# Attention scores of two heads in the two row halves of the TensorE array, with one PSUM bank left for transpositions

## The chip, the cores and the metric

The kernel runs on one core of a Trainium2 chip, as one program with one launch. The metric is the time of an execution on the device in microseconds (us), lower is better. Engines are named as in the profile: PE is TensorE's matmul, PEld its weight load, DVE is VectorE, ACT is ScalarE, POOL is GpSimd and SP is SyncE, which issues the DMAs.

## The reference, cut to what matters

The program is one layer of a diffusion backbone: 1024 latent tokens and 256 context tokens of width 1024 go through an input projection into two token mixers (a bidirectional mLSTM and windowed attention), a gated merge, and a ConvFFN. The change is in the attention:

```python
# 16 query heads, 4 key/value heads, head width 64; blocks of T = 128 queries
s_lat = einsum('btkgd,bskd->bkgts', qblk, kblk) * ATT_SCALE   # 3 blocks of keys around the query block
s_lat = where(valid, s_lat, NEG_INF)                          # |i - j| <= 128
s_ctx = einsum('btkgd,bskd->bkgts', qblk, k_ctx) * ATT_SCALE  # all 256 context keys
p = softmax(concatenate([s_lat, s_ctx, sink_b], axis=-1))[..., :3*T + C]
out = p_lat @ v_lat + p_ctx @ v_ctx
```

## The kernel before

Everything is fp32. A product of two fp32 matrices is made from rounded parts: a value x is split into a high part that the matmul takes exactly (type fp32r) and the remainder, and the products of the parts are added up. In most of the kernel that is three products (high by high, high by low, low by high; `mm3`, L95 to L97 and `filler`, L692).

**The attention's loop.** 32 blocks (4 key/value heads g, 8 query blocks b each) go through a software pipeline, one step n for each. A step issues `proj` of block n (24 products, 384 columns, tile `pq`), `stacks` of block n-1 (transposes q and k, tile `qt`), `scores` of block n-3 (tile `s`), and `pv` of block n-4. `filler` gives each step 24 products of 512 columns of another projection (tile `g`), which need nothing from the attention, and which are put between the steps' other products. The order on each engine is made by a list scheduler when the program is built, not by the order of the source.

**Scores.** The head width is 64, so `stacks` puts the high part of q into one half of the 128 rows and the low part into the other half (`QT`, four heads of 128 columns), while the keys stand twice, once in each half (`KA` the high parts, `KB` the low parts; `KcA` and `KcB` for the context). A matmul over all 128 rows then gives (high q + low q) by one part of the keys, and two of them give all four products. Per head:

```python
595  for h in range(4):
596      ps = s_tile(f"s{n}_{h}")
597      q = QT[:, h * P : (h + 1) * P]
599          nc.tensor.matmul(ps[:, off:512], q, KA[:, b0 * P : b1 * P], start=True, stop=False)
600          nc.tensor.matmul(ps[:, off:512], q, KB[:, b0 * P : b1 * P], start=False, stop=True)
601          nc.tensor.matmul(ps[:, 512 : 512 + NCTX], q, KcA[:, g], start=True, stop=False)
602          last = nc.tensor.matmul(ps[:, 512 : 512 + NCTX], q, KcB[:, g], start=False, stop=True)
```

The latent keys are 384 columns wide (256 in the first and the last block of a head group), the context keys 256. One DVE instruction per head then scales, masks and finds the maximum (L606, reading `s` from PSUM), ACT takes the exponential (L610), and POOL normalises (L619).

**Probabilities by values.** `pv` transposes the probabilities of four heads for one block of 128 keys into one PSUM bank (four matmuls against the identity, L639, tile `pt`); `split_from` copies the bank to `ph` on ACT (L44) and subtracts on DVE to get `pl` (L49); both must have read the bank before it can be written again. Then two products (L633 with `ph`, L634 with `pl`) add to `po`. A block has five such key blocks (four at the ends).

**PSUM.** There are eight banks of 512 columns. Before, `mm_tile` has two, `fl_tile` (the filler) one, `tp_tile` (all transpositions: `qt`, `pt`, and a small one for the modulation, `ms`) three, and `s_tile` two, which hold one head's scores.

Of the kernel before, what the change touches and what calls it, by code (L numbers as in the profile page):

```python
# [8 lines left out]
F32 = mybir.dt.float32  # L9
F32R = mybir.dt.float32r  # L10
AF = mybir.ActivationFunctionType
ALU = mybir.AluOpType
# [87 lines left out]
def sl(a, n):  # L100
    return slice(a, a + n)
# [3 lines left out]
def layer_kernel(ctx: ExitStack, tc: tile.TileContext, A: dict, out: bass.AP, dbg=None):  # L105
# [28 lines left out]
    pss = psx_s.enter_context(tc.tile_pool(name="ps_s", bufs=1, space=PSUM, reuse_waits="tile"))  # L134
    ph1 = ExitStack()
# [12 lines left out]

    def tp_tile(name):
        return pst.tile([P, 512], F32, tag="tp", name=name)  # L150

    def s_tile(name):
        return pss.tile([P, 1024], F32, tag="s", name=name)

# [5 lines left out]
        attT_d=attT_d, mlT_d=mlT_d, sga_d=sga_d, sgm_d=sgm_d, kx_d=kx_d, vx_d=vx_d, sil3=sil, sil=sil[:, :, 0], dbg=dbg,  # L160
        mm_tile=mm_tile, fl_tile=fl_tile, tp_tile=tp_tile, s_tile=s_tile, psx_s=psx_s,
# [82 lines left out]
def attention_setup(E, st):  # L244
    nc, tc, A = E.nc, E.tc, E.A
    ap = st.enter_context(tc.tile_pool(name="at1", bufs=1, reuse_waits="tile"))
    at = Ctx()
    maskA = ap.tile([P, 640], F32, name="maskA")
    mask7 = ap.tile([P, 512], F32, name="mask7")
    nsink = ap.tile([P, 16], F32, name="nsink")  # L250
# [9 lines left out]
    def tables(cs):  # L260
        nc.sync.dma_start(cs, A["rope"].rearrange("(b p) c -> p b c", p=P))
        nc.sync.dma_start(sink, A["sink"].to_broadcast([P, 16]))
        nc.sync.dma_start(E.gb, A["gate_b"].to_broadcast([P, 16]))
        nc.sync.dma_start(maskA, A["maskA"])
        nc.sync.dma_start(mask7, A["mask7"])
# [12 lines left out]
    Vc = ap.tile([P, NCB, NKV, P], F32R, name="Vc")  # L278
    at.__dict__.update(maskA=maskA, mask7=mask7, nsink=nsink, sink=sink, qw=qw, TA=TA, TB=TB, KcA=KcA, KcB=KcB, Vc=Vc, constants=constants, tables=tables)
    return at  # L280
# [221 lines left out]
def stage_attention(E, st, at):  # L502
    nc, tc, A, ident, expo, hT, wts, vecT = E.nc, E.tc, E.A, E.ident, E.expo, E.hT, E.wts, E.vecT
    mm_tile, tp_tile, s_tile, attT_d = E.mm_tile, E.tp_tile, E.s_tile, E.attT_d
    maskA, mask7, nsink, sink, TA, TB = at.maskA, at.mask7, at.nsink, at.sink, at.TA, at.TB
    KcA, KcB, Vc = at.KcA, at.KcB, at.Vc
# [51 lines left out]
    def stacks(g, b):  # L558
        n = f"{g}_{b}"
        qf, ss = S1.pop((g, b))  # L560
        kf = wp.tile([P, 2, HD], F32, tag="kf", name=f"kf{n}", bufs=2)
        nc.vector.tensor_scalar(kf, qf[:, None, 256:320].to_broadcast([P, 2, HD]), ss[:, 4:5], None, op0=ALU.mult)


        pt = tp_tile(f"qt{n}")
        for i in range(2):
            nc.tensor.transpose(pt[:, i * P : (i + 1) * P], qf[:, i * P : (i + 1) * P], ident)
        nc.tensor.transpose(pt[:, 256:384], kf.rearrange("p r d -> p (r d)"), ident)
        QT = wp.tile([P, 512], F32R, tag="QT", name=f"QT{n}", bufs=3)
        Q4 = QT.rearrange("p (i r t) -> p r i t", i=2, r=2)  # L570
        pq = pt[:, 0:256].rearrange("p (i t) -> p i t", i=2)
        halves = slice(0, HD), slice(HD, P)
# [5 lines left out]
        for r in range(2):  # L578
            hi, lo = halves[r], halves[1 - r]
            nc.vector.tensor_tensor(Q4[lo, r], pq[hi], Q4[hi, r].bitcast(F32), op=ALU.subtract)  # L580
        nc.vector.tensor_tensor(G[g]["KB"][:, ts], pt[:, 256:384], G[g]["KA"][:, ts].bitcast(F32), op=ALU.subtract)
        S2[(g, b)] = (QT, ss)

    def scores(g, b):
# [4 lines left out]
        W = nl + NCTX  # L589
        off = 512 - nl  # L590
        mask = maskA[:, 128:640] if b == 0 else (mask7 if b == NB - 1 else maskA)
        KA, KB = G[g]["KA"], G[g]["KB"]
        st4 = wp.tile([P, 16], F32, tag="st", name=f"st{n}", bufs=4)
        Ps, prior = [], None
        for h in range(4):
            ps = s_tile(f"s{n}_{h}")
            q = QT[:, h * P : (h + 1) * P]
            with behind(prior):
                nc.tensor.matmul(ps[:, off:512], q, KA[:, b0 * P : b1 * P], start=True, stop=False)
                nc.tensor.matmul(ps[:, off:512], q, KB[:, b0 * P : b1 * P], start=False, stop=True)  # L600
                nc.tensor.matmul(ps[:, 512 : 512 + NCTX], q, KcA[:, g], start=True, stop=False)
                last = nc.tensor.matmul(ps[:, 512 : 512 + NCTX], q, KcB[:, g], start=False, stop=True)  # L602
            prior = FILL.products(6) if h in (0, 1, 2) else None
            pm = pp.tile([P, 640], F32, tag="P", name=f"P{n}_{h}", bufs=8)
            hh = 4 * g + h
            nc.vector.tensor_tensor_reduce(  # L606
                pm[:, :W], ps[:, off : off + W], mask[:, :W], scale=ss[:, h : h + 1], scalar=nsink[:, hh : hh + 1],
                op0=ALU.add, op1=ALU.min, accum_out=st4[:, h : h + 1],
            )
            nc.scalar.activation(  # L610
                pm[:, :W], pm[:, :W], AF.Exp, bias=st4[:, h : h + 1], scale=-1.0, accum_out=st4[:, 4 + h : 5 + h]
            )
            Ps.append(pm)
        nc.vector.tensor_tensor(st4[:, 8:12], st4[:, 0:4], sink[:, 4 * g : 4 * g + 4], op=ALU.add)
# [3 lines left out]
        for h in range(4):  # L618
            nc.gpsimd.tensor_scalar(Ps[h][:, :W], Ps[h][:, :W], st4[:, 12 + h : 13 + h], 1.0, op0=ALU.mult, op1=ALU.mult)  # L619
        S3[(g, b)] = (Ps, b0, b1)  # L620

    def pv(g, b):
# [13 lines left out]
        for kb in range(nk):  # L636
            pt = tp_tile(f"pt{n}_{kb}")
            for h in range(4):
                turned = nc.tensor.transpose(pt[:, h * P : (h + 1) * P], Ps[h][:, kb * P : (kb + 1) * P], ident)  # L639
            ph = pp.tile([P, 512], F32R, tag="ph", name=f"ph{n}_{kb}", bufs=3)  # L640
# [93 lines left out]
def stage_mlstm(E, st):  # L734
    nc, tc, A, ident, expo, hT, wts, dr = E.nc, E.tc, E.A, E.ident, E.expo, E.hT, E.wts, E.dr
    mm_tile, tp_tile, s_tile, mlT_d, gtile = E.mm_tile, E.tp_tile, E.s_tile, E.mlT_d, E.gtile

    E.psx_s.close()
    psd = E.psx_s.enter_context(tc.tile_pool(name="ps_d", bufs=2, space=PSUM, reuse_waits="tile"))
    E.d_tile = lambda name: psd.tile([P, 512], F32, tag="d", name=name)  # L740
    mp = st.enter_context(tc.tile_pool(name="ml1", bufs=1, reuse_waits="tile"))
# [248 lines left out]
    def states(h):  # L990
# [5 lines left out]
        def update(d, i, c):  # L996
# [7 lines left out]
            nc.vector.scalar_tensor_tensor(kl, ks[c], wk, kh.bitcast(F32), op0=ALU.mult, op1=ALU.subtract)  # L1004
            pd = psd.tile([P, 512], F32, tag="d", name=f"dC{nm}")
            mm3(nc, pd[:, :DVA], [(kh, kl)], [VA[c]], sl(0, P), sl(0, DVA))
# [160 lines left out]
def stage_tail(E, st):  # L1167
# [342 lines left out]

    psc = E.psx_s
    U = Units(
# [16 lines left out]
    with tc.issue_after(held.ins):  # L1529
        w = load_w(A["w_o"][1], "wo1", g1b[:, 512:1024], raws=raw)  # L1530
    E.psx_s.close()
    psc = st.enter_context(tc.tile_pool(name="ps_c", bufs=2, space=PSUM, reuse_waits="tile"))
    E.c_tile = lambda n: psc.tile([P, 512], F32, tag="C", name=n)
    for b in range(4):
# [397 lines left out]
def host_arrays(inp):  # L1932
# [56 lines left out]
    z = np.zeros((P, P))  # L1989
    a["maskA"] = np.concatenate([prev, z, nxt, z, z], axis=1).astype(np.float32)  # L1990
    a["mask7"] = np.concatenate([prev, z, z, z], axis=1).astype(np.float32)
    fw = np.where(i[:, None] <= i[None, :], 0.0, NEG)
# [21 lines left out]
```

## Time and profile before

| | us |
|---|---|
| median of 3 runs | 1909.65 (1908.51 to 1911.2) |
| the profiled execution, its own time | 1909.96 |
| its span in the trace | 1908.2 |
| attention's stretch of the span (all 32 blocks) | about 130 to 640 |

The span is what the trace shows between the first and the last instruction; the execution's own time is 1.76 us longer. A timeline row has its start (us from the span's start), its length, engine, line, operation, the tile written and those read, and a count where rows were merged (then the length is that of all of them). Matmuls overlap: the distance between two starts is what one costs, and the length of one is longer.

### The profile page before, as it was taken

To read this page: it belongs to the slowest core of one execution; us is meant where nothing else is said; L and a number is where in the kernel's file an instruction comes from. 1 tells how busy PE (TensorE), PEld (TensorE's weight loads), DVE (VectorE), ACT (ScalarE), POOL (GpSimd) and SP (SyncE) were. 2 spreads that over 40 slices of the span, in tenths; PEclk is the share of its full clock that TensorE was granted. 3 is DMA by queue.
4 is the path that set the end of the run, shared out by engine and by line. 5 is a ranking of instruction groups with operands and counts; after the bars stand their busy time and mean duration, and the time that the engine had idled before them with its cause. 6 is when DMAs were issued, how large, how long until landed. Compare 5 with 4: busy or idle time off the path is not lost.

```text
span 1908.2 us, 28768 instructions
## 1 busy us (share of the span) xinstructions
PE 1880.6 (99%) x10021; PEld 1631.5 (86%) x10021; DVE 1434.3 (75%) x2892; ACT 998.1 (52%) x1984; POOL 306.5 (16%) x524
## 2 busy tenths in 40 slices
PE   7999999999999999999999999999999999999999
PEld 3898888989888899999988887888888888888887
DVE  3767878877677766667577878679888889897565
ACT  4845656555556445454546665276544444455441
POOL 1223333333333231212020012000000000000000
PEclk9999999999999999999999999999999999999999
DMA  9632222322122433435318973613355444499851
GB/s 355 197 121 75 67 72 67 103 61 84 59 64 83 129 92 119 133 125 166 133 56 291 383 263 127 237 67 110 135 201 188 185 165 174 164 320 347 305 165 67
DMA packets 139570, 298.54 MB, mean 156 GB/s; under 512 B 15504, under 2 KB 39968, under 8 KB 136608
## 3 DMA queue, kind: packets, MB, share of 16 engines
q1 hardware_dynamic: 125024, 270.48, 40.9%
q10 hardware_dynamic: 14400, 26.22, 4.0%
q8 instruction: 79, 1.29, 0.3%
q14 instruction: 67, 0.55, 0.1%
HBM read 220.55 MB, written 76.10 MB: 155 GB/s over the span
## 4 chain that ended last, share of the span: by engine, by line
PE 89%; DVE 4%; ACT 2%; DMA 2%; POOL 2%; issue 1%; POOLq 0%; SPq 0%; ACTq 0%; DVEq 0%
PE g L692 9%; PE pa L1591 4%; PE pa L1593 4%; PE pa L1592 4%; PE pt L639 3%; PE pq L95 2%; PE pq L96 2%; PE yb L1593 2%; PE yb L1592 2%; PE pq L97 2%; PE yb L1591 2%; PE kv L96 2%; PE kv L95 2%; PE kv L97 2%; PE dx L1593 2%; PE po L633 2%
## 5 line engine op out<-in xcount | busy, mean ns | idle before, releaser
L619 POOL TENSOR_SCALAR P<-P,st 128x640 f32<-128x640 f32 (+1 forms) x128 | 106.7, 852 | 222.6 <-DVE st L617 80.3
L610 ACT ACTIVATE P<-P,st 128x640 f32<-128x640 f32 (+1 forms) x128 | 102.8, 803 | 58.6 <-DVE st L606 58.6
L606 DVE CUSTOM_DVE_ANT_0 P<-s,maskA,nsink 128x640 f32<-128x640 f32 (+1 forms) x112 | 103.0, 920 | 22.2 <-PE s L602 20.6
L49 DVE TENSOR_TENSOR pl<-pt,ph 128x512 fp32r<-128x512 f32 x152 | 100.6, 684 | 4.5 <-ACT ph L44 3.3
L44 ACT ACTIVATE ph<-pt 128x512 fp32r<-128x512 f32 x152 | 86.2, 595 | 30.9 <-PE pt L639 29.5
L692 PE MATMUL g<-hH,fh 128*128 128x512 f32 x256 | 101.2, 395 | 0.0
L692 PE MATMUL g<-hH,fl 128*128 128x512 f32 x256 | 100.6, 393 | 0.0
L692 PE MATMUL g<-hL,fh 128*128 128x512 f32 x256 | 100.2, 391 | 0.0
L95 PE MATMUL pq<-w1h,hH 128*128 128x384 f32 (+1 forms) x256 | 87.0, 340 | 0.1
L97 PE MATMUL pq<-w1h,hL 128*128 128x384 f32 (+1 forms) x256 | 86.9, 339 | 0.0
L639 PE MATMUL pt<-ident,P 128*128 128x128 f32 x608 | 86.4, 272 | 0.3 <-POOL P L619 0.3
L96 PE MATMUL pq<-w1l,hH 128*128 128x384 f32 (+1 forms) x256 | 86.4, 338 | 0.0
L639 PEld LDWEIGHTS pt<-ident,P 128*128 128x128 f32 x608 | 72.3, 140 | 10.0 <-POOL P L619 0.5
L95 PE MATMUL mo<-w1h,hH 128*128 128x256 f32 x256 | 72.0, 281 | 0.0
L1729 ACT ACTIVATE cv<-ua,vecT 128x1024 f32<-128x1024 f32 x22 | 27.4, 1244 | 85.0 <-DVE ua L1702 85.0
L97 PE MATMUL mo<-w1h,hL 128*128 128x256 f32 x256 | 71.8, 280 | 0.0
L96 PE MATMUL mo<-w1l,hH 128*128 128x256 f32 x256 | 71.8, 280 | 0.0
L1003 POOL TENSOR_SCALAR kwh<-k,gcall 128x128 fp32r<-128x128 f32 x72 | 32.4, 454 | 237.6 <-PE dC L96 189.0
L96 PE MATMUL kv<-w1l,hH 128*128 128x384 f32 x208 | 70.2, 338 | 0.0
L97 PE MATMUL kv<-w1h,hL 128*128 128x384 f32 x208 | 70.0, 337 | 0.0
L95 PE MATMUL kv<-w1h,hH 128*128 128x384 f32 x208 | 70.0, 337 | 0.0
L1591 PE MATMUL dx<-dwh,dfh 128*128 128x512 f32 (+1 forms) x176 | 68.3, 388 | 0.0
(600 smaller groups left out, 6405.1 us busy)
## 6 DMA issues: line engine op xcount, KB each, us to landing
ur<-in_w_up SPq DMA_DIRECT2D x22, 1024.0 KB, 4.9
wmb<-in_w_modB SPq DMA_DIRECT2D x48, 256.0 KB, 2.8
f_d<-cv SPq DMA_DIRECT2D x22, 512.0 KB, 2.6
wm<-in_w_modA SPq DMA_DIRECT2D x16, 512.0 KB, 10.2
fr<-in_w_g SPq DMA_DIRECT2D x32, 256.0 KB, 3.1
drf<-fs_d SPq DMA_DIRECT2D x15, 512.0 KB, 7.1
drw<-wt_d SPq DMA_DIRECT2D x14, 512.0 KB, 6.4
w1b<-in_w_cx SPq DMA_DIRECT2D x16, 388.0 KB, 5.1
```

What stands on the lines that cost most here:

```text
L49: rest = nc.vector.tensor_tensor(lo, src, hi.bitcast(F32), op=ALU.subtract)
L95: nc.tensor.matmul(ps, lh[:, ls], rh[:, rs], start=start and i == 0, stop=False)
L96: nc.tensor.matmul(ps, lh[:, ls], rl[:, rs], start=False, stop=False)
L97: nc.tensor.matmul(ps, ll[:, ls], rh[:, rs], start=False, stop=stop and i == n - 1)
L606: nc.vector.tensor_tensor_reduce(pm[:, :W], ps[:, off : off + W], mask[:, :W], scale=ss[:, h : h + 1], scalar=nsink[:, hh : hh + 1], op0=A ...
L610: nc.scalar.activation(pm[:, :W], pm[:, :W], AF.Exp, bias=st4[:, h : h + 1], scale=-1.0, accum_out=st4[:, 4 + h : 5 + h])
L619: nc.gpsimd.tensor_scalar(Ps[h][:, :W], Ps[h][:, :W], st4[:, 12 + h : 13 + h], 1.0, op0=ALU.mult, op1=ALU.mult)
L639: turned = nc.tensor.transpose(pt[:, h * P : (h + 1) * P], Ps[h][:, kb * P : (kb + 1) * P], ident)
L692: return lambda: nc.tensor.matmul(ps, w, x, start=i == 0, stop=i == len(todo) - 1)
L1591: nc.tensor.matmul(ps, lh, rh, start=start and i == 0, stop=False, skip_group_check=True)
L1592: nc.tensor.matmul(ps, lh, rl, start=False, stop=False, skip_group_check=True)
L1593: nc.tensor.matmul(ps, ll, rh, start=False, stop=stop and i == n - 1, skip_group_check=True)
```

## The change

`QT` now holds the high parts of all four heads (columns 0 to 255) and their low parts (256 to 511), with head 2i in rows 0 to 63 and head 2i+1 in rows 64 to 127. One ACT copy and one DVE subtraction over 128 rows make it, where there were two of each over 64 rows. A score matmul is over 64 rows: head 2i uses rows 0 to 63 of the array, head 2i+1 rows 64 to 127. Each head has three products per key part (low by low is left out), so a pair of heads has 12 matmuls, which alternate between the two halves, where two heads had 8 over 128 rows. The two heads write to different banks: `s_tile` is now four banks, for a pair. `tp_tile` is left with one bank in the attention; outside of it the two banks that this frees are a second pool (`third`), and `tp_tile` turns through three banks as before. The order of the key parts in the first and the last block, and the masks (one table for two), are changed to suit. The filler is given out 12 products after the first pair, where it was six after each of three heads.

```diff
-    pst = psx.enter_context(tc.tile_pool(name="ps_tp", bufs=3, space=PSUM, reuse_waits="tile"))
+    pst = psx.enter_context(tc.tile_pool(name="ps_tp", bufs=1, space=PSUM, reuse_waits="tile"))
...
+    def banks(tag, n, bufs, third):
+        psx_s.close()
+        pool = psx_s.enter_context(tc.tile_pool(name=f"ps_{tag}", bufs=bufs, space=PSUM, reuse_waits="tile"))
+        setattr(PS, tag, lambda name: pool.tile([P, n], F32, tag=tag, name=name))
+        PS.third, PS.turn = None, 0
+        if third:
+            PS.third = psx_s.enter_context(tc.tile_pool(name=f"ps_{tag}t", bufs=2, space=PSUM, reuse_waits="tile"))
...
+            banks("s", 2048, 1, False)
             stage_attention(E, st, at)
...
-        for r in range(2):
-            hi, lo = halves[r], halves[1 - r]
-            copy_act(nc, Q4[hi, r], pq[hi])
+        copy_act(nc, QT[:, 0:256], pt[:, 0:256])
...
-        for h in range(4):
-            ps = s_tile(f"s{n}_{h}")
-            q = QT[:, h * P : (h + 1) * P]
+        for i in range(2):
+            ps = s_tile(f"s{n}_{i}")
+            work = []
+            for r, (al, ac, _) in enumerate(places):
+                rows = sl(r * HD, HD)
+                qh, ql = QT[rows, sl(i * P, P)], QT[rows, sl(256 + i * P, P)]
+                both = []
+                for at_, w, (ka, kb) in (
+                    (al, nl, (KA[rows, lat], KB[rows, lat])),
+                    (ac, NCTX, (KcA[rows, g], KcB[rows, g])),
+                ):
+                    both.append([(ps[:, at_ : at_ + w], q, k) for q, k in ((qh, ka), (ql, ka), (qh, kb))])
+                work.append(both[0] + both[1])
             with behind(prior):
-                nc.tensor.matmul(ps[:, off:512], q, KA[:, b0 * P : b1 * P], start=True, stop=False)
...
+                for j in range(6):
+                    for r in range(2):
+                        o, q, k = work[r][j]
+                        nc.tensor.matmul(o, q, k, start=j % 3 == 0, stop=j % 3 == 2)
-            prior = FILL.products(6) if h in (0, 1, 2) else None
+            prior = FILL.products(12) if i == 0 else None
```

The scheduler makes a new order from this. In the rows below `s_3_0` is the first tile of scores of query block 3 of the third head group (before: its first head; now: its first pair), `pt_2_1` the transposed probabilities of query block 2 for its second block of keys, `ph` and `pl` their two parts, `g` the filler and `pq` the next projection.

On PE, before, from the last transposition of the first key block on: with three banks the sets of transpositions stand side by side.

```order
L639 MATMUL pt_2_0_5093<-ident,P_2_3_4892 128x128
L639 MATMUL pt_2_1_5102<-ident,P_2_0_4856 128x128
L639 MATMUL pt_2_1_5102<-ident,P_2_1_4870 128x128
L639 MATMUL pt_2_1_5102<-ident,P_2_2_4884 128x128
L639 MATMUL pt_2_1_5102<-ident,P_2_3_4892 128x128
L639 MATMUL pt_2_2_5111<-ident,P_2_0_4856 128x128
L639 MATMUL pt_2_2_5111<-ident,P_2_1_4870 128x128
L639 MATMUL pt_2_2_5111<-ident,P_2_2_4884 128x128
L639 MATMUL pt_2_2_5111<-ident,P_2_3_4892 128x128
L633 MATMUL po_2_5092<-ph_2_0_5098,V_3850 128x512
L599 MATMUL s_3_3_5076<-KA_3848,QT_3_4640 128x384
L600 MATMUL s_3_3_5076<-KB_3849,QT_3_4640 128x384
```

On PE, in the changed kernel, the same place: the second pair's twelve products stand between two sets (`x4` is two heads, high and low part of q; `x2` is two heads).

```order
L665 MATMUL pt_2_0_5169<-ident,P_2_3_4964 128x128
L718 MATMUL g_1_5108<-hH_93,fh_4905 128x512
L718 MATMUL g_1_5108<-hL_101,fh_4905 128x512
L623 MATMUL s_3_1_5141<-KA_3902,QT_3_4710 128x384 x4
L623 MATMUL s_3_1_5141<-KB_3903,QT_3_4710 128x384 x2
L623 MATMUL s_3_1_5141<-KcA,QT_3_4710 128x256 x4
L623 MATMUL s_3_1_5141<-KcB,QT_3_4710 128x256 x2
L665 MATMUL pt_2_1_5178<-ident,P_2_0_4942 128x128
```

The sets are now kept apart by two filler products and one pair of heads. Of the 64 pairs in the program, 54 stand in one piece like this one; the other ten are cut up by products over all 128 rows, into 28 pieces.

On PE, in the changed kernel, from the fourth to the fifth key block of the same query block:

```order
L665 MATMUL pt_2_3_5198<-ident,P_2_3_4964 128x128
L658 MATMUL po_2_5168<-pl_2_2_5193,V_3904 128x512
L97 MATMUL pq_7_5249<-w1h_3880,hL_97 128x384
L95 MATMUL pq_7_5249<-w1h_3880,hH_90 128x384
L96 MATMUL pq_7_5249<-w1l_3881,hH_90 128x384
L657 MATMUL po_2_5168<-ph_2_3_5203,Vc 128x512
L97 MATMUL pq_7_5249<-w1h_3880,hL_98 128x384
L95 MATMUL pq_7_5249<-w1h_3886,hH_91 128x384
L96 MATMUL pq_7_5249<-w1l_3887,hH_91 128x384
L665 MATMUL pt_2_4_5209<-ident,P_2_0_4942 128x128
```

Before, only the two `po` products stood there; now six `pq` products have been moved in between.

On DVE, before, between the second and the third subtraction from a bank of transpositions:

```order
L606 ISA P_3_2_5073,st_3_5033<-s_3_2_5062,maskA,nsink,ss_3_4433 128x640
L606 ISA st_3_5033 128x1
L49 TENSOR_TENSOR pl_2_0_5099<-pt_2_0_5093,ph_2_0_5098 128x512
L49 TENSOR_TENSOR pl_2_1_5108<-pt_2_1_5102,ph_2_1_5107 128x512
L606 ISA P_3_3_5081,st_3_5033<-s_3_3_5076,maskA,nsink,ss_3_4433 128x640
L606 ISA st_3_5033 128x1
L49 TENSOR_TENSOR pl_2_2_5117<-pt_2_2_5111,ph_2_2_5116 128x512
```

On DVE, in the changed kernel, the same place (L630 is the line of the masking instruction now):

```order
L49 TENSOR_TENSOR pl_2_0_5175<-pt_2_0_5169,ph_2_0_5174 128x512
L630 ISA P_3_2_5154,st_3_5109<-s_3_1_5141,mask,nsink,ss_3_4499 128x640
L630 ISA st_3_5109 128x1
L630 ISA P_3_3_5157,st_3_5109<-s_3_1_5141,mask,nsink,ss_3_4499 128x640
L630 ISA st_3_5109 128x1
L49 TENSOR_TENSOR pl_2_1_5184<-pt_2_1_5178,ph_2_1_5183 128x512
```

Both masking instructions of the second pair now stand ahead of the subtraction that frees the one bank; before, one stood between two subtractions, and two other banks were there.

More of the change, by code (lines that the diff above doesn't have):

```diff
@@ L149, in tp_tile @@
     def tp_tile(name):
+        PS.turn += 1
+        if PS.third is not None and PS.turn % 3:
+            return PS.third.tile([P, 512], F32, tag="tq", name=name)
         return pst.tile([P, 512], F32, tag="tp", name=name)
     def s_tile(name):
-        return pss.tile([P, 1024], F32, tag="s", name=name)
+        return PS.s(name)
     kx_d = dr.tile([NCB, P, MLH * DQK], F32, name="kx_d")
@@ L247, in attention_setup @@
     at = Ctx()
-    maskA = ap.tile([P, 640], F32, name="maskA")
-    mask7 = ap.tile([P, 512], F32, name="mask7")
+    mask = ap.tile([P, 7 * P], F32, name="mask")
     nsink = ap.tile([P, 16], F32, name="nsink")
@@ L263, in tables @@
         nc.sync.dma_start(E.gb, A["gate_b"].to_broadcast([P, 16]))
-        nc.sync.dma_start(maskA, A["maskA"])
-        nc.sync.dma_start(mask7, A["mask7"])
+        nc.sync.dma_start(mask, A["mask"])
         nc.gpsimd.tensor_scalar(nsink, sink, -1.0, 1.0, op0=ALU.mult, op1=ALU.mult)
@@ L278, in attention_setup @@
     Vc = ap.tile([P, NCB, NKV, P], F32R, name="Vc")
-    at.__dict__.update(maskA=maskA, mask7=mask7, nsink=nsink, sink=sink, qw=qw, TA=TA, TB=TB, KcA=KcA, KcB=KcB, Vc=Vc, constants=constants, tables=tables)
+    at.__dict__.update(mask=mask, nsink=nsink, sink=sink, qw=qw, TA=TA, TB=TB, KcA=KcA, KcB=KcB, Vc=Vc, constants=constants, tables=tables)
     return at
@@ L504, in stage_attention @@
     mm_tile, tp_tile, s_tile, attT_d = E.mm_tile, E.tp_tile, E.s_tile, E.attT_d
-    maskA, mask7, nsink, sink, TA, TB = at.maskA, at.mask7, at.nsink, at.sink, at.TA, at.TB
+    mask, nsink, sink, TA, TB = at.mask, at.nsink, at.sink, at.TA, at.TB
     KcA, KcB, Vc = at.KcA, at.KcB, at.Vc
@@ L569, in stacks @@
         QT = wp.tile([P, 512], F32R, tag="QT", name=f"QT{n}", bufs=3)
[L570 to L575 removed]
+        copy_act(nc, QT[:, 0:256], pt[:, 0:256])
         ts = sl(b * P, P)
         copy_act(nc, G[g]["KA"][:, ts], pt[:, 256:384])
[L578 to L580 removed]
+        nc.vector.tensor_tensor(QT[:, 256:512], pt[:, 0:256], QT[:, 0:256].bitcast(F32), op=ALU.subtract)
         nc.vector.tensor_tensor(G[g]["KB"][:, ts], pt[:, 256:384], G[g]["KA"][:, ts].bitcast(F32), op=ALU.subtract)
@@ L589, in scores @@
         W = nl + NCTX
-        off = 512 - nl
-        mask = maskA[:, 128:640] if b == 0 else (mask7 if b == NB - 1 else maskA)
+        lat = sl(b0 * P, nl)
         KA, KB = G[g]["KA"], G[g]["KB"]
+        if b == 0:
+            places = ((0, nl, 384), (1024, 1024 + nl, 384))
+        elif b == NB - 1:
+            places = ((NCTX, 0, 0), (1024 + NCTX, 1024, 0))
+        else:
+            places = ((512 - nl, 512, 256), (1536 - nl, 1536, 256))
         st4 = wp.tile([P, 16], F32, tag="st", name=f"st{n}", bufs=4)
@@ L594, in scores @@
         Ps, prior = [], None
-        for h in range(4):
-            ps = s_tile(f"s{n}_{h}")
-            q = QT[:, h * P : (h + 1) * P]
-            with behind(prior):
[L599 to L602, printed above, removed]
-            prior = FILL.products(6) if h in (0, 1, 2) else None
[L604 to L613, printed above, removed]
+        for i in range(2):
[11 more added lines that the diff above has]
+                work.append(both[0] + both[1])
+            with behind(prior):
+                for j in range(6):
[3 more added lines that the diff above has]
+            prior = FILL.products(12) if i == 0 else None
+            for r, (al, ac, m) in enumerate(places):
+                h = 2 * i + r
+                a = min(al, ac)
+                pm = pp.tile([P, 640], F32, tag="P", name=f"P{n}_{h}", bufs=8)
+                hh = 4 * g + h
+                nc.vector.tensor_tensor_reduce(
+                    pm[:, :W], ps[:, a : a + W], mask[:, m : m + W], scale=ss[:, h : h + 1], scalar=nsink[:, hh : hh + 1],
+                    op0=ALU.add, op1=ALU.min, accum_out=st4[:, h : h + 1],
+                )
+                nc.scalar.activation(
+                    pm[:, :W], pm[:, :W], AF.Exp, bias=st4[:, h : h + 1], scale=-1.0, accum_out=st4[:, 4 + h : 5 + h]
+                )
+                Ps.append((pm, 0 if al < ac else NCTX, 0 if ac < al else nl))
@@ L638, in pv @@
             for h in range(4):
-                turned = nc.tensor.transpose(pt[:, h * P : (h + 1) * P], Ps[h][:, kb * P : (kb + 1) * P], ident)
+                p, lat, ctx = Ps[h]
+                at_ = lat + kb * P if kb < b1 - b0 else ctx + (kb - (b1 - b0)) * P
+                nc.tensor.transpose(pt[:, h * P : (h + 1) * P], p[:, at_ : at_ + P], ident)
             ph = pp.tile([P, 512], F32R, tag="ph", name=f"ph{n}_{kb}", bufs=3)
@@ L1530, in stage_tail @@
         w = load_w(A["w_o"][1], "wo1", g1b[:, 512:1024], raws=raw)
-    E.psx_s.close()
-    psc = st.enter_context(tc.tile_pool(name="ps_c", bufs=2, space=PSUM, reuse_waits="tile"))
-    E.c_tile = lambda n: psc.tile([P, 512], F32, tag="C", name=n)
+    E.banks("c", 512, 2, True)
+    E.c_tile = E.PS.c
     for b in range(4):
@@ L1989, in host_arrays @@
     z = np.zeros((P, P))
-    a["maskA"] = np.concatenate([prev, z, nxt, z, z], axis=1).astype(np.float32)
-    a["mask7"] = np.concatenate([prev, z, z, z], axis=1).astype(np.float32)
+    a["mask"] = np.concatenate([z, z, prev, z, nxt, z, z], axis=1).astype(np.float32)
     fw = np.where(i[:, None] <= i[None, :], 0.0, NEG)
```

16 lines of the change are left out of this document (8 added, 8 removed).

## The prediction

> **What bounds the kernel now.** I read the page first, then the attention's stretch by windows, then PE's waits in that stretch, then single blocks in the timeline.
>
> ```profile
> span 1908.2 us, 28768 instructions
> PE 1880.6 (99%) x10021; PEld 1631.5 (86%) x10021; DVE 1434.3 (75%) x2892; ACT 998.1 (52%) x1984; POOL 306.5 (16%) x524
> 130.00:640.00 510.00, 508.48 (x2927) 453.17 (x2926) 385.82 (x978) 299.82 (x688) 177.27 (x252) 1.00 0.23 70
> PEld s L599 <- DVE st L606: 2.6, 9, 0.9
> PEld po L633 <- ACT ph L44: 2.2, 6, 0.6
> PEld po L634 <- DVE pl L49: 2.1, 7, 0.4
> ```
>
> The first two rows are of the page, the third is the attention's window (PE, PEld, DVE, ACT, POOL, then the granted clock), the last three are PE's longest waits in it. PE is busy for 508.48 of 510 us, and waits for DVE or ACT for 2 to 3 us in a group. So PE is the bound: a shorter row of products shortens the program, and whatever makes PE wait lengthens it at full price. The profiled execution took 1909.96 us against the median of 1909.65, so I count from 1910. A difference of 0.2% (3.8 us) is about what a measurement of this kernel can tell from none.
>
> **What the scores cost now.** Timeline of PE, one head inside a group, then one head of an end block, then neighbours of other kinds. The distance of two starts is the price.
>
> ```profile
> 312.53 0.33 PE L599 MATMUL s<-KA,QT 128*128 128x384 f32 x1
> 312.70 0.34 PE L600 MATMUL s<-KB,QT 128*128 128x384 f32 x1
> 312.87 0.28 PE L601 MATMUL s<-KcA,QT 128*128 128x256 f32 x1
> 312.99 0.28 PE L602 MATMUL s<-KcB,QT 128*128 128x256 f32 x1
> 313.11 0.39 PE L634 MATMUL po<-pl,V 128*128 128x512 f32 x1
> ...
> 505.07 0.28 PE L599 MATMUL s<-KA,QT 128*128 128x256 f32 x1
> 505.54 0.39 PE L692 MATMUL g<-hH,fh 128*128 128x512 f32 x1
> ...
> 309.12 0.39 PE L692 MATMUL g<-hL,fh 128*128 128x512 f32 x1
> 309.35 0.39 PE L692 MATMUL g<-hH,fl 128*128 128x512 f32 x1
> ...
> 311.17 1.14 PE L639 MATMUL pt<-ident,P 128*128 128x128 f32 x9
> ```
>
> 384 columns cost 0.17, 256 cost 0.12, 512 cost 0.23, and a transposition (1.14 - 0.27)/8 = 0.11. An inner head costs 0.58, an end head 0.47; two heads 1.16 and 0.94.
>
> **The gain, if the halves run side by side.** Then a pair has six steps of two matmuls, each as long as one: 3 x 0.17 + 3 x 0.12 = 0.87 inside a group, 6 x 0.12 = 0.72 at its ends. Of the 64 pairs, 48 are inner (24 blocks) and 16 at the ends: 48 x 0.29 + 16 x 0.22 = 17.4 us less. The trace has no two row halves at work together. The nearest is two strips of columns, in the start-up:
>
> ```profile
> 21.20 0.49 PE L358 MATMUL xct<-ident,x 128*128 128x128 f32 x3
> 21.62 0.60 PE L373 MATMUL pm<-wm,sil 128*2 128x512 f32 x2
> L373 PE MATMUL pm<-wm,sil x64: 591/592/1061, 5.6 to 29.4; 128*2 128x512 f32 x64
> ```
>
> Two `pm` matmuls, written to different strips of 32 columns, take 0.60 together where one takes 0.592: the array does run two at once. I take the full overlap. The other bound is none, or weight loads that don't overlap (below, among the rivals).
>
> **What entering and leaving the halves costs.** The array now changes between 128 rows and twice 64. The start-up has changes of shape: from transpositions over 2 rows (`pmT`) to 128 rows, and the one above, into column strips. In mid-attention there is a small transposition with 8 weight columns (`gT`).
>
> ```profile
> 31.11 0.38 PE L336 MATMUL pmT<-ident,mrow 2*128 2x2 f32 x4
> 20.35 0.32 PE L336 MATMUL pmT<-ident,mrow 2*128 2x2 f32 x3
> 20.59 0.44 PE L358 MATMUL xct<-ident,x 128*128 128x128 f32 x2
> 31.43 0.50 PE L95 MATMUL pkc<-w1h,hcH 128*128 128x256 f32 x2
> ...
> 257.00 0.34 PE L95 MATMUL pq<-w1h,hH 128*128 128x384 f32 x1
> 257.17 0.34 PE L96 MATMUL pq<-w1l,hH 128*128 128x384 f32 x1
> 257.35 0.27 PE L238 MATMUL gT<-ident,m 128*8 128x128 f32 x1
> 257.37 0.42 PE L97 MATMUL pq<-w1h,hL 128*128 128x384 f32 x1
> 257.63 0.33 PE L95 MATMUL pq<-w1h,hH 128*128 128x384 f32 x1
> ```
>
> One `pmT` costs 0.38 - 0.32 = 0.06, so the last of the four starts at 31.29, and `pkc` follows 0.14 later, 0.07 late. Then its two matmuls take 0.50, where two of 256 columns take 0.12 + 0.28 = 0.40: the second waited 0.10, for a weight load that could not be made ahead. Together 0.17. Into transpositions it is less: the last `pmT` starts at 20.47, `xct` at 20.59 (0.06 late), and two take 0.44 instead of 0.38: 0.12. Into column strips: the third `xct` starts at 21.42, `pm` at 21.62, 0.20 later instead of 0.11: 0.09, with weights of two columns only. Against this, `gT` and the `pq` after it take 0.28 from start to start, which is 0.11 + 0.17: no cost at all.
>
> I take 0.17 into the halves (weights as wide as `pkc`'s) and 0.12 out of them, 0.29 for a visit, since `pmT` is the row that changes the rows of the array, as this does; `gT` changes only columns. By the new order the 64 pairs stand in 54 + 28 = 82 pieces: 82 x 0.29 = 23.8 us more; bounds 0 (`gT`) and 82 x 0.34 = 27.9.
>
> [...]
>
> **What one bank costs.** Before, three sets of transpositions could stand ahead of their readers. Now each set must be read by ACT, then DVE, before the next. The turn with the least delay in the trace, and how fast PE goes on after DVE:
>
> ```profile
> 636.68 0.60 PE L639 MATMUL pt<-ident,P 128*128 128x128 f32 x4
> 637.31 0.60 ACT L44 ACTIVATE ph<-pt 128x512 fp32r<-128x512 f32 x1 [0.68 <-PE pt L639]
> 637.94 0.69 DVE L49 TENSOR_TENSOR pl<-pt,ph 128x512 fp32r<-128x512 f32 x1 [0.46 <-ACT ph L44]
> ...
> 594.54 0.68 DVE L49 TENSOR_TENSOR pl<-pt,ph 128x512 fp32r<-128x512 f32 x1
> 595.28 0.50 PE L634 MATMUL po<-pl,V 128*128 128x512 f32 x1
> ```
>
> The set of four ends its row at 636.68 + 4 x 0.11 = 637.12, DVE is done with the bank at 638.63, and PE needs 595.28 - 595.22 = 0.06 to go on. PE therefore needs 1.51 + 0.06 = 1.57 us of other work between two sets, or it waits. I went through all 123 such stretches of the new order with the prices above:
> - About 36 hold two `po` and six `pq` (or three `g` and two `pq`), as the order's third place does: 2 x 0.23 + 6 x 0.17 = 1.48, with the finer spacing 1.50. Short by 0.07; and since a transposition that had to wait has its load exposed (0.06, the `xct` row), 0.13 each: 4.7 us.
> - 17 hold two `g` and one pair: 0.46 + 0.87 + 0.29 = 1.62, just enough, so nothing. Without the 0.29 they would be short by 0.24.
> - Some ten hold a cut pair, with at least two visits; enough, or nearly so.
> - Four at the end, where filler and `pq` have run out, hold two or three `po` and little else (0.46, 0.46, 0.69, 0.93): 3.7 us.
>
> Sum 8.4 us. It is a lower bound of the turns, since ACT and DVE must be free when a set is ready; the upper bound is a rival below.
>
> **Smaller edits.** One ACT copy instead of two, one DVE subtraction instead of two in `stacks`:
>
> ```profile
> L44 ACT ACTIVATE QT<-qt x60: 366/378/383, 132.4 to 602.1; 64x256 fp32r<-64x256 f32 x60
> L580 DVE TENSOR_TENSOR QT<-qt,QT x60: 417/422/427, 135.2 to 603.4; 64x256 fp32r<-64x256 f32 x60
> ```
>
> That frees about 0.38 and 0.42 per block on engines that are idle for about a quarter of the stretch (DVE) or more (ACT); PE gets it only where it waits, and the qt bank has long covers (2 us and more of products behind it). The mask as one DMA, the pools outside the attention (three banks in turn, as before) and the second pair's wait for both heads' masking (12 `g`, 2.8 us, against two maskings of 0.94) I count at nothing; if the last cover went, it would be 0.3 us or so for each block without filler, of which there are three.
>
> **The sum.** -17.4 + 23.8 + 8.4 = +14.8 on 1910: 1925 us. With other prices of a visit and delays in the queues, 1916 to 1937.
>
> **The rivals.**
> - *The visits are free* (the `gT` row) and the halves overlap: -17.4. But then the 17 stretches with two `g` and a pair are short by 0.24 + 0.06 each, 5.1 us, and the ten with cut pairs by some 0.35 each, 3.5: the bank gives 17 back. 1910, and 1901 if those ten and the exposed loads cost nothing. It ends at no change or a little faster; it decides wherever a `g` is followed by a score matmul 0.23 later.
> - *The halves don't run side by side.* If only the weight loads follow each other, at the 0.10 that `pkc` shows, a pair takes 12 x 0.105 = 1.26: 48 x 0.10 + 16 x 0.32 = +9.9 instead of -17.4, so 1952. If the matmuls do, 1.74 and 1.44: 48 x 0.58 + 16 x 0.50 = +35.8, so 1978. Against it stand the `pm` rows, whose loads are only two columns wide. [...]
> - *The bank is the bound in every block.* In the new order DVE masks both heads of the second pair ahead of the subtraction that frees the bank.
>
> ```profile
> L606 DVE CUSTOM_DVE_ANT_0 P<-s,maskA,nsink 128x640 f32<-128x640 f32 x96 | 90.1, 939 | 19.7 <-PE s L602 18.2 <-PE pt L639 1.1
> ```
>
> If one masking more than I allow for (0.94) lies on that turn in each of 32 blocks, 30 us are added: 1955. For it: DVE is the busiest after PE. Against it: the stretch behind it is among the longest (seven `g` and three `po`, 2.3 us).
>
> **Chances and range.** My forecast has 0.43, free visits 0.30, no overlap 0.16 (half for each kind), the bank in every block 0.11. The likeliest is 1925. Leaving out matmuls that follow each other (0.08), the lowest of the free visits (0.06) and the upper part of the last rival (0.05) gives 1904 to 1955. Faster by over 0.2% is most of free visits, where some turns cost less than I have it: 0.20. Within it: 0.08 of that case and 0.05 of my forecast: 0.13. Slower: 0.38 of my forecast, 0.02 of free visits, 0.16 and 0.11: 0.67.
>
> **What would show it.** In the changed profile the two score matmuls of a step should start within 0.01 of each other and the next step 0.12 or 0.17 later; a score matmul after a `g` should start about 0.32 after it and not 0.23; `pt` should appear among PE's waits, for `pl` on DVE, with 5 to 10 us in all, the longest near 640. The forecast is wrong if the steps are 0.21 or more apart (no overlap), if the start after a `g` is on time (free visits), or if waits for `pl` come to 30 us (the bank).

## The result and the profile after

| | us |
|---|---|
| before, median of 4 runs on this chip | 1910.2 |
| after, median of 4 runs | 1953.14 (1951.18 to 1954.57) |
| ratio, 95% interval | 1.0225 (1.0212 to 1.0238) |
| the profiled execution after: own time, span | 1953.03, 1951.2 |

The kernel is 43 us slower; 15 had been forecast. One of the four executions of e4 below took 6431.42 us at a granted clock of 0.33 and is left out of its time; all others are in the fast state. First the page after (its size and PE's busy time), then the attention's stretch, which now ends near 690 and not near 640, by windows (PE, PEld, DVE, ACT, POOL, granted clock):

```profile
span 1951.2 us, 29310 instructions
PE 1916.3 (98%) x10277; PEld 1607.7 (82%) x10277; DVE 1422.1 (73%) x2860; ACT 987.0 (51%) x1952; POOL 308.3 (16%) x524
130.00:690.00 560.00, 550.50 (x3215) 434.28 (x3213) 381.14 (x957) 292.08 (x663) 179.03 (x258) 0.99 0.23 70
```

The page has PE at 98% (99% before), and DVE, ACT and POOL are busy for about as long as before. In the stretch PE is idle for 9.5 us where it was idle for 1.5. That accounts for little of the loss, because a stretched matmul counts as busy (the `po` at 346.31 below lasts 0.50, one that did not wait, at 349.39, 0.39): the loss is in the distances between starts and in what the weight loads wait for. PEld's waits in the same stretch (what is loaded, what it waits for, us in total, times, longest):

```profile
PEld po L657 <- ACT ph L44: 38.6, 120, 1.8
PEld pt L665 <- DVE pl L49: 14.4, 53, 0.5
PEld s L623 <- issue: 13.3, 59, 0.4
PEld s L623 <- PE pt L665: 6.2, 18, 0.4
```

The first of these was 2.2 us before. It says that `po` stands in the weight queue for ACT's copy of the transpositions, in 120 of its 152 products with `ph`. A load's wait overlaps with matmuls already under way (the load of the `po` at 346.31 waits 0.31, while the `pq` of 345.99 runs for 0.33), so these 38.6 us are not all lost; the next timelines show what is. First PE around one pair of heads:

```profile
337.61 0.48 PE L718 MATMUL g<-hH,fh 128*128 128x512 f32 x1
337.92 0.40 PE L718 MATMUL g<-hL,fh 128*128 128x512 f32 x1
338.25 0.61 PE L623 MATMUL s<-KA,QT 64*128 64x384 f32 x4
338.70 0.33 PE L623 MATMUL s<-KB,QT 64*128 64x384 f32 x2
338.87 0.40 PE L623 MATMUL s<-KcA,QT 64*128 64x256 f32 x4
...
334.20 0.28 PE L623 MATMUL s<-KcB,QT 64*128 64x256 f32 x2
334.42 0.50 PE L718 MATMUL g<-hH,fh 128*128 128x512 f32 x1
334.75 0.39 PE L718 MATMUL g<-hL,fh 128*128 128x512 f32 x1
```

The two matmuls of a step take the time of one: `KB` x2 start at 338.70 and the next step at 338.87, 0.17 later. A visit costs four pieces of 0.10. The first score matmul starts 0.33 after a `g` and not 0.23; the first two steps take 0.45 and not 0.35; the first `g` starts 0.22 after the last step and not 0.12; the second `g` comes 0.33 after the first and not 0.23. Together 0.40.

Now a tight stretch between two sets of transpositions, PE first, then ACT's copy of the set that starts at 344.96:

```profile
344.96 0.60 PE L665 MATMUL pt<-ident,P 128*128 128x128 f32 x4
345.32 0.48 PE L658 MATMUL po<-pl,V 128*128 128x512 f32 x1
345.63 0.34 PE L96 MATMUL pq<-w1l,hH 128*128 128x384 f32 x1
345.81 0.34 PE L97 MATMUL pq<-w1h,hL 128*128 128x384 f32 x1
345.99 0.33 PE L95 MATMUL pq<-w1h,hH 128*128 128x384 f32 x1
346.31 0.50 PE L657 MATMUL po<-ph,Vc 128*128 128x512 f32 x1
346.65 0.34 PE L96 MATMUL pq<-w1l,hH 128*128 128x384 f32 x1
...
345.66 0.60 ACT L44 ACTIVATE ph<-pt 128x512 fp32r<-128x512 f32 x1 [0.61 <-PE pt L665]
```

ACT is done with `ph` at 346.26 and `po` starts at 346.31, 0.32 after the `pq` ahead of it instead of 0.17. The `pq` behind it then comes 0.34 later instead of 0.23: its weight load comes behind `po`'s own, which stood waiting until 346.31, and starts at 346.42, 0.11 after `po`, where the next `pq`'s load starts with the matmul ahead of it (both at 346.65). So this one stall costs 0.15 + 0.11, with ACT idle for 0.61 until the set was ready.

I added up these excesses over all of PE's distances, from the first `pq` to the last `pt`, each against the usual distance of its kind. That stretch is 545.0 us before and 591.4 after; 13 `kv` and 3 `po` products more lie in it, 2.9 us, which leaves 43.5:

| us | forecast | by the trace |
|---|---|---|
| steps of two matmuls for one | -17.4 | -17.4 |
| 82 visits | +23.8 | +32 (0.39 each) |
| `pt` waits for the bank | +8.4 | +8 |
| `po` waits for ACT's `ph` | 0 | +11 |
| loads exposed behind a `po` that had to wait (`pq`, `g`, `kv`) | 0 | +12 |
| scores no longer wait for DVE | 0 | -3 |

The last four rows are sums over stalls of 0.1 to 0.3, and a stall at a pair's edge is split between two rows by its usual price (0.09 to leave), so each is good to 1 us or so, the clock aside.

Some 3 us of these rows, an estimate, are the clock. Behind several waits of PE, 2.2 us in all from 670 to 678, 6.8 us at the end of the attention ran at a granted clock of 0.50 (677.8 to 684.6). There the starts behind a `kv` of 384 columns stand 0.32 apart and not 0.17, and those behind a product of 512 columns 0.43 and not 0.23. Before, the whole attention ran at a granted clock of 1.00.

### The profile page after: what moved, and what is told of

Its sections match the earlier page's. It is cut to its first block, busy times and chain, and to the rows that moved or that the text cites. A ratio compares the mean times of both kernels' runs of the same rounds, so it can differ in the third digit from the quotient of the medians.

```text
span 1951.2 us, 29310 instructions
## 1 busy us (share of the span) xinstructions
PE 1916.3 (98%) x10277; PEld 1607.7 (82%) x10277; DVE 1422.1 (73%) x2860; ACT 987.0 (51%) x1952; POOL 308.3 (16%) x524
## 4 chain that ended last, share of the span: by engine, by line
PE 84%; DVE 7%; ACT 4%; issue 2%; DMA 2%; POOL 2%; SPq 0%; POOLq 0%; ACTq 0%; DVEq 0%
PE g L718 7%; PE pa L1614 4%; PE pa L1616 4%; PE pa L1615 4%; PE pt L665 4%; PE po L657 3%; PE yb L1615 2%; PE yb L1616 2%; PE yb L1614 2%; PE pq L97 2%; PE pq L96 2%; PE kv L95 2%; PE kv L96 2%; PE pq L95 2%; PE kv L97 2%; PE dx L1616 2%
## 5 line engine op out<-in xcount | busy, mean ns | idle before, releaser
L49 DVE TENSOR_TENSOR pl<-pt,ph 128x512 fp32r<-128x512 f32 x152 | 104.7, 689 | 91.4 <-ACT ph L44 91.1
L44 ACT ACTIVATE ph<-pt 128x512 fp32r<-128x512 f32 x152 | 90.5, 595 | 124.5 <-PE pt L665 124.1
L630 DVE CUSTOM_DVE_ANT_0 P<-s,mask,nsink 128x640 f32<-128x640 f32 (+1 forms) x128 | 111.3, 905 | 6.3 <-PE s L623 3.8
L718 PE MATMUL g<-hH,fh 128*128 128x512 f32 x256 | 106.1, 415 | 0.9 <-ACT fo L44 0.9
L665 PE MATMUL pt<-ident,P 128*128 128x128 f32 x608 | 95.8, 280 | 2.9 <-DVE pl L49 1.4
L665 PEld LDWEIGHTS pt<-ident,P 128*128 128x128 f32 x608 | 70.4, 141 | 26.0 <-DVE pl L49 14.4
L1616 PE MATMUL dx<-dwh,dfl 128*128 128x512 f32 (+1 forms) x176 | 68.2, 388 | 0.0
```

The source lines that it names most:

```text
L49: rest = nc.vector.tensor_tensor(lo, src, hi.bitcast(F32), op=ALU.subtract)
L630: nc.vector.tensor_tensor_reduce(pm[:, :W], ps[:, a : a + W], mask[:, m : m + W], scale=ss[:, h : h + 1], scalar=nsink[:, hh : hh + 1], op ...
L665: nc.tensor.transpose(pt[:, h * P : (h + 1) * P], p[:, at_ : at_ + P], ident)
L718: return lambda: nc.tensor.matmul(ps, w, x, start=i == 0, stop=i == len(todo) - 1)
L1616: nc.tensor.matmul(ps, ll, rh, start=False, stop=stop and i == n - 1, skip_group_check=True)
```

## Experiments

The theory to test: one bank for transpositions costs about 28 us by the table, most of it not at `pt` but at `po`; a visit costs 0.40; the halves do overlap. The rivals: the loss belongs to the halves (dearer visits, or matmuls that don't overlap everywhere), or the bank alone is the whole of it. Before stood at 1909.12 in the runs of e1 to e4 and at 1909.28 in those of e5 to e8.

**e1: the change without the halves.** Banks, pairs and masks as after, `QT` and the score matmuls over 128 rows as before.

```diff
-    both.append([(ps[:, at_ : at_ + w], q, k) for q, k in ((qh, ka), (ql, ka), (qh, kb))])
+    both.append([(ps[:, at_ : at_ + w], q, k) for k in (ka, kb)])
...
-                for j in range(6):
-                    for r in range(2):
+                for r in range(2):
+                    for j in range(4):
```

> The changed kernel with its banks, its pairs and its order of the filler, but scores over all 128 rows as before (q stacked high over low, two products per key part, eight matmuls per pair). Theory (the changed trace: steps of two halves start together, -17 us; a visit to the halves costs 0.39 us, 82 visits 32 us; the rest of the +43 is PE waiting in the stretches of the one bank): taking the halves away gives 15 us back, 1935 to 1942. Rival one (the halves are a gain, the bank alone is the loss): 17 us slower than the change, about 1970. Rival two (the halves are the whole loss): 1910.

Measured 1957.97, ratio 1.0253 (1.0238 to 1.0268). PEld's first wait:

```profile
PEld po L663 <- ACT ph L44: 46.6, 138, 2.0
```

The theory missed. Without any visit the kernel is no faster but 5 us slower than with the halves. So the first two rows of the table (+15) can't simply be taken off: the waits are larger here. By PE's distances the waits over those of before are about 29 us in the change (43.5 + 17.4 - 32) and 47 here. Part of this is the clock: in the profiled execution 20.5 us of the attention ran at a granted clock of 0.50, where the change has 6.8. The longest such stretch (as a window), and two `g` of the other one, 0.42 apart instead of 0.23:

```profile
669.90:687.00 17.10, 14.96 (x43) 10.30 (x44) 7.90 (x15) 4.70 (x10) 3.79 (x14) 0.50 0.54 181
202.77 0.63 PE L724 MATMUL g<-hL,fh 128*128 128x512 f32 x1
203.19 0.63 PE L724 MATMUL g<-hH,fl 128*128 128x512 f32 x1
```

By such distances that is about 7 us against 3, so most of the 5 us is the clock. The other 14 us of new waits are about what the halves cost in the table (15). The scheduler made another order as well: 26 stretches between two sets hold two `po` and six `pq`, where the change has 17. How much of the 14 is the missing visits and how much the order is not shown.

**e2: the kernel before with one bank.** Head by head and over 128 rows; in the attention `tp_tile` has one bank, two banks stay unused.

```diff
-    pst = psx.enter_context(tc.tile_pool(name="ps_tp", bufs=3, space=PSUM, reuse_waits="tile"))
+    pst = psx.enter_context(tc.tile_pool(name="ps_tp", bufs=1, space=PSUM, reuse_waits="tile"))
```

> The kernel before, head by head over 128 rows and with two score banks, but with one bank for transpositions in the attention (three outside of it); two banks stay empty. Theory: the waits for ph and for the bank come with the one bank alone, 22 to 32 us over before, 1932 to 1942. Rival two (the visits are all): 1908 to 1915. Rival one (the bank is all of the +43 and what the halves save besides): 1953 to 1970.

Measured 1953.36, ratio 1.0231 (1.0216 to 1.0246). PEld's waits:

```profile
PEld po L648 <- ACT ph L44: 32.3, 106, 1.1
PEld s L614 <- DVE st L621: 10.8, 36, 1.0
PEld pt L654 <- DVE pl L49: 6.7, 24, 0.5
```

The theory's 1932 to 1942 missed, and this is the rival's end: the bank alone costs 44 us, with the new order that comes with it, as much as the whole change. The wait of `po` for ACT is there without any row halves. Here PE also waits for DVE's masking of scores (10.8), since scores still have two banks, and `g` waits for ACT's reading of its own bank (5.4).

**e5: the kernel before with two banks**, as e2, with one bank unused.

> As the kernel before, head by head over 128 rows, but with two banks for transpositions in the attention (one bank alone gave 1953). Theory now (the +43 is the waiting of po, pt and the scores behind one bank, which ACT and DVE must both read before it is free): a second bank lets one set be read while the next is made, so nearly all comes back, 1910 to 1920. Rival (something else in the pools costs it, such as the switch between the attention and the stages around it): 1940 or more.

Measured 1920.32, ratio 1.0061 (1.0046 to 1.0076). PEld's waits:

```profile
PEld po L648 <- ACT ph L44: 12.3, 32, 1.0
PEld s L614 <- DVE st L621: 5.0, 14, 0.9
PEld pt L654 <- DVE pl L49: 2.3, 7, 0.9
```

Three banks, two, one: 1909, 1920, 1953. The second bank taken away costs three times the first, and at each step `po` leads the waits, not `pt`.

**e3: `po` held back.** The change, with the products of a key block kept behind the transpositions of the next one; only the order of PE changes.

```diff
-            if kb >= 2:
-                values(kb - 2)
-        values(nk - 2)
+            if kb >= 1:
+                values(kb - 1, turned)
```

> The change, but the two products po of a key block are held behind the transpositions of the next key block, so that ACT's and DVE's reading of the bank has all the filler between two sets as its cover. Theory (each po with ph stands too early, waits 0.15 for ACT's copy and then has its load exposed by 0.10): 12 to 18 us faster than the change, 1935 to 1941. Rival (that wait only moves to the bank, whose turn is the limit): 1950 to 1955.

Measured 1944.08, ratio 1.0182 (1.0167 to 1.0197). PEld's waits:

```profile
PEld pt L665 <- DVE pl L49: 28.9, 75, 2.4
...
PEld po L657 <- ACT ph L44: 7.5, 29, 0.6
```

The wait of `po` falls from 38.6 to 7.5, and 9 us are won, a little less than expected. The rest moved. A stretch between two sets holds as many products as before, since a `po` of the set before takes the place of the early one, and PE is through them sooner: with two `po` and six `pq` it goes from set to set in 2.13 instead of 2.24 (medians of 16 and 17 stretches). Then `pt` waits for DVE's reading of the bank, 75 times instead of 53, and 28.9 us instead of 14.4. So the place of `po` explains some 9 of the bank's price; what is left is the turn itself, and no order seen here hides it.

**e4: more visits.** The change, with one `g` put between a pair's latent and context parts where filler remains: 137 visits instead of 82.

```diff
+            with behind(FILL.products(1, last)):
+                for j in range(3, 6):
```

> The change, but between the latent and the context products of a pair one filler product is put, so that the new order has 137 visits to the halves instead of 82; nothing else is added. Theory (0.39 a visit): +21 us less up to 3 for longer covers, 1971 to 1975. Rival (0.29 a visit as forecast): +16, 1966 to 1970. Rival (visits free, as with the transposition of 8 weight columns): no change, 1950 to 1956.

Measured 1983.73 (three executions), ratio 1.0384 (1.0363 to 1.0405): 31 us more, 0.56 for each further visit, and above the 1971 to 1975 expected. A cut pair in PE's timeline:

```profile
346.77 0.34 PE L623 MATMUL s<-KB,QT 64*128 64x384 f32 x2
347.04 0.50 PE L723 MATMUL g<-hH,fh 128*128 128x512 f32 x1
347.47 0.50 PE L628 MATMUL s<-KcA,QT 64*128 64x256 f32 x4
347.81 0.28 PE L628 MATMUL s<-KcB,QT 64*128 64x256 f32 x2
```

From `KB` to the `g` 0.27 and not 0.17; from the `g` to the scores 0.43 and not 0.23, since a lone `g` has its own load exposed too (among PEld's waits `g` stands 42 times there, 10.3 us in all, and twice in the change, 1.6); two steps of `KcA` in 0.34 and not 0.23. That makes 0.40 for a cut, 22 for 55 of them. The rest is 9 us by the medians and 12 in the profiled execution. Most of it is the clock: five stretches of that execution's attention, 30.6 us in all, ran at a granted clock of 0.50. By the distances there they lose about 11 us, an estimate, against 3 in the change. So a visit's own price is near 0.40, and the 0.29 was too low.

**e6: the halves not in turn.** The change, with the six matmuls of one half first, then the six of the other.

```diff
-                for j in range(6):
-                    for r in range(2):
+                for r in range(2):
+                    for j in range(6):
```

> The change, but a pair's twelve matmuls in another order: six of the first half, then six of the second, instead of alternating. Theory: the halves run side by side only when their matmuls alternate; without it a pair takes 0.87 more inside a group and 0.72 more at its ends, 53 us of PE time, of which the longer cover gives back up to 15: 1990 to 2006. Rival (the two halves overlap through the queue whatever the order): 1950 to 1958. Rival (the loads are the limit, 0.105 each): 1965 to 1975.

Measured 1976.16, ratio 1.0351 (1.0334 to 1.0369), 23 us more than the change. An inner pair:

```profile
341.46 0.61 PE L623 MATMUL s<-KA,QT 64*128 64x384 f32 x2
341.91 0.33 PE L623 MATMUL s<-KB,QT 64*128 64x384 f32 x1
341.92 0.44 PE L623 MATMUL s<-KA,QT 64*128 64x384 f32 x1
342.08 0.40 PE L623 MATMUL s<-KcA,QT 64*128 64x256 f32 x2
342.20 0.33 PE L623 MATMUL s<-KA,QT 64*128 64x384 f32 x1
342.32 0.28 PE L623 MATMUL s<-KcB,QT 64*128 64x256 f32 x1
342.37 0.33 PE L623 MATMUL s<-KB,QT 64*128 64x384 f32 x1
342.54 0.40 PE L623 MATMUL s<-KcA,QT 64*128 64x256 f32 x2
342.78 0.28 PE L623 MATMUL s<-KcB,QT 64*128 64x256 f32 x1
342.99 0.50 PE L718 MATMUL g<-hH,fh 128*128 128x512 f32 x1
```

The pair takes 1.53 from its first start to the `g`, where the change takes 1.09 (333.33 to 334.42) and twelve matmuls after each other would take 1.96 by estimate (1.74 at the prices of before, and the 0.22 to the `g`). The overlap is thus what the change's alternation brings, as the theory has it, but the loss is half of what was expected: the second half begins (341.92, `KA`) while the first still has its `KcA` and `KcB` (342.08 to 342.32) ahead of it in the program. The time is 1 us above the rival of loads (1965 to 1975), but the rows don't bear it out: with loads one after the other at the rival's 0.105, two starts of one half with a start of the other between them would stand 0.21 apart, and here they stand 0.17 apart (341.91 to 342.08 with 341.92 between).

**e7 and e8: halves with three banks.** Full-size scores of a pair take four banks. With fewer context keys a pair fits in two, and three are left for transpositions. e7 is the kernel before with these keys, e8 the change with them.

```diff
-        W = nl + NCTX
+        W = nl + P
...
-            places = ((0, nl, 384), (1024, 1024 + nl, 384))
+            places = ((0, nl, 384), (512, 512 + nl, 384))
```

> The kernel before with 128 of the 256 context keys left out in the attention (scores, softmax and values), so that one head's scores fit one bank. It is the base for the next kernel. Theory and rivals alike: one set of four transpositions and two products po fewer per block, 0.9 us x 32, and a little from shorter scores: 1870 to 1885.

> The change with the same 128 context keys left out: a pair's scores fit two banks, so three banks stay for transpositions. Its order has 64 visits to the halves. Theory (a pair is 0.28 us shorter side by side but a visit costs 0.39, and with three banks there is no waiting): 64 x 0.11 = 7 us slower than the kernel with the same keys left out over 128 rows, between 3 and 12. Rival (visits free): 17 us faster. Rival (waits come with the pairs and not with the bank): 30 us slower or more.

Measured 1892.60 for e7, ratio 0.9916 (0.9901 to 0.9931), and 1911.45 for e8, ratio 1.0009 (1.0000 to 1.0019): the halves cost 18.85 us here. Both are slower than expected. The leading waits of e7, then of e8, then a pair of e8 with the masking it waits for:

```profile
PEld s L599 <- DVE st L606: 18.6, 51, 1.3
```

```profile
PEld s L623 <- issue: 33.3, 60, 2.7
PEld po L658 <- DVE pl L49: 10.9, 33, 1.0
...
312.05 0.62 PE L623 MATMUL s<-KA,QT 64*128 64x384 f32 x4 [0.46 <-DVE st L630]
...
311.08 0.81 DVE L630 CUSTOM_DVE_ANT_0 P<-s,mask,nsink 128x512 f32<-128x512 f32 x1
```

With three banks `po` waits for ACT for only 3.0 us in 11 times, but the second pair waits for DVE to finish masking the first (PE is idle for 0.46 ahead of 312.05), since both pairs share two banks. By PE's distances scores start 24.9 us late in e8; 64 entries at 0.10 are 6.4 of that, so 18 are waiting. The halves' own account is 64 x 0.40 = 25.6 for visits less 17.1 for steps (48 x 0.28 + 16 x 0.23, at 0.17, 0.12 and 0.11 a step), +8.5. The other 10 are put down to the scarce score banks, some 3 of them by way of the clock (two stretches of 3.4 us at 0.50 in e8's attention, none in e7's). The experiment therefore doesn't give the price of the halves free of any bank's price; it shows that the change loses whichever tiles are short of banks.

## Why the prediction was wrong

- **PE is the bound, and its waits count in full**: right: the stalls of PE are on the path (its distances grow by 43.5 us, the time by 43), and that is how the bank's price reached the time.
- **The halves run side by side, -17.4**: right. Steps start 0.17 and 0.12 apart; the rival without overlap is out, and e6 shows what happens without the alternation.
- **A visit, 0.29**: right in kind, too small. It measured 0.39 to 0.40, 32 us instead of 23.8. The way in was taken at 0.17 and measured 0.20; the way out was taken from `xct`, 0.12, where only 0.06 of a load is exposed, and measured 0.20 into a `g`: two pieces of 0.10, as on the way in.
- **What one bank costs, 8.4**: the step that failed. I asked whether PE has 1.57 us of other work between two sets, counted `po` as such work, and so found only the stretches where `pt` comes too early. That part came out as said (8). But a `po` with `ph` in that stretch isn't free work: it needs ACT's copy of the set just ahead of it, and stands before that copy is there. That is 11 us, and 12 more for the loads behind it: 28 us in all with `pt` and the scores, and 44 when the bank is taken away alone (e2). Of the 23, e3 wins back 9 by placing `po` later; then PE waits for the bank itself. The turn was not the error: 2.01 us from set to set by the forecast's rows (0.44 and 1.57), 2.07 where the change has three `g`, two `po` and two `pq` between two sets (median of 14). The prediction held ACT's and DVE's readiness as the risk; it was the order of PE's own queue. Before, a `po` could stand right behind a set of transpositions, since it read an earlier one, as PE's timeline before has it:

```profile
511.20 0.60 PE L639 MATMUL pt<-ident,P 128*128 128x128 f32 x4
511.55 0.48 PE L633 MATMUL po<-ph,V 128*128 128x512 f32 x1
```

This `po` starts 0.35 after the set's first transposition, when a copy that takes 0.60 can't be there.
- **The bank in every block (+30, 1955)**: nearest in size, with another mechanism than the one written there. The masking of two heads ahead of the subtraction would show as waits for `pl`; these are 14.4 in 53 stalls, none over 0.5. The waits for `ph` are the large ones. That 1953 lies within the stated 1904 to 1955 is luck: the upper end is this rival's, and the forecast's own mechanism was given 1916 to 1937.
- **Terms added as if independent**: e1, e2 and the change stand at 1958, 1953 and 1953. The bank alone (+44) and the change (+43) cost the same, so the +15 of the halves does not come on top of the bank's price. That a visit lengthens stretches in which PE would wait otherwise would explain it, and the prediction saw this for 17 stretches of two `g` and a pair; but e1 and e2 have other orders too, so it is argued and not shown. Against e1 the halves are worth 5 us, most of it the clock; in e8, with three banks, they are a loss.
- **The clock**: the prediction has no term for it. It is 3 us of the 43 by the estimate above, so it doesn't decide the case.

No version here that keeps all keys beats the kernel before. A visit shared by both pairs of a block would save 32 of them, some 13 us at 0.40 by estimate, but with full-size scores it needs eight banks for them, and no run tests it.

## What to carry to other kernels

Before a buffer is taken from a pipeline, list for every instruction between two uses of it not only how long it takes but what it waits for: a consumer of what was just put into the buffer is no cover for it, while one of the set before is (e3, 9 us won). A small stall of PE, whose loads are made ahead, was paid twice here, once as the wait (11 us for `po`) and once as the next load, which is exposed (12 us). And weigh packing by the piece: here two matmuls side by side won 0.29 in an inner pair, and each visit, into the halves and out again, took 0.40. Read the granted clock beside the waits: e1 and e4 looked like dearer waits until the stretches at 0.50 were taken out.

## What the runs showed of the hardware that I had not expected

- In e6 matmuls on different row halves start out of the order of the program: the second half's first matmul starts at 341.92, ahead of three matmuls of the first half (342.08 to 342.32) that stand before it.
- Behind a stalled `po` of the change the next product starts about 0.1 late (346.31 to 346.65 is 0.34 instead of 0.23), and a lone `g` between two visits starts 0.10 late and is followed 0.20 late (0.27 and 0.43 in e4).
- The granted clock fell to 0.50 for 3.4 to 17.1 us at a time in the attention of the change, e1 to e4, e6 and e8, whose profiled executions have a mean clock of 0.991 to 0.997, and not in that of the kernel before, e5 and e7 (1.00 from 130 to 640 in each). In the change the stretch stands right behind waits of PE of 2.2 us in all (670 to 678, for ACT's `ph` and DVE's `pl`); no run here isolates what sets such a stretch off.
